# Expert stage: residual and pair sums on TensorE, weights split 2048 columns at a time

## The chip, the cores and the metric

The kernel runs on one core of one Trainium2 chip. The metric is device time in microseconds of one execution; several executions are timed and the median is given. PE is TensorE, DVE is VectorE, ACT is ScalarE, POOL is GpSimd, SP is SyncE, which here issues the loads of weights.

## The reference

A block of two layers on x of 256 tokens x 1024 channels, in float32. Each layer adds a mixer (retention, latent attention, mLSTM), then a feed-forward part, each with a residual and a layer norm. The second layer's feed-forward part is a mixture of 8 experts, of which each token takes 2:

```python
logits = (t @ router).astype(jnp.float32)
top_v, top_i = lax.top_k(logits, TOP_K)
top_w = jax.nn.softmax(top_v, axis=-1)
gate = jnp.sum(jax.nn.one_hot(top_i, N_EXPERTS) * top_w[..., None], axis=1)
y = jnp.zeros((bsz * s, d), jnp.float32)
for e in range(N_EXPERTS):
    y = y + gate[:, e:e + 1] * swiglu(t, wg[e], wu[e], wd[e])
...
x = layer_norm(DN_ALPHA * x + f, ln2_w[l], ln2_b[l])
```

swiglu is (silu(x @ wg) * (x @ wu)) @ wd with a hidden width of 3584. The experts' weights are 352 MB in float32. Everything else is small beside them.

## The kernel before, in words

**Numbers in two parts.** PE multiplies fp32r values. To keep float32's precision each operand is split into a high part (a cast to fp32r, by ACT) and a low part (operand minus high part, by DVE). A product is then three matmuls (`mm3`, L374: high x high, high x low, low x high). Where an expert has at most 64 tokens, high and low part of the activations stand side by side in the 128 columns of one stationary operand, and two matmuls do (`products`, L1544, the branch at L1564); a small matmul (`fold_in`, L1590) then adds the low half to the high one. Which of the two ways an expert takes is decided on the chip by its token count.

**Weights.** A piece is 128 partitions x 2048 columns (1 MB), loaded by SP into a raw place. `piece` (L313) returns a function `half(i)` that splits 1024 of its columns: one ACT cast (L347) and one DVE subtract (L348) into a pair of places from `next_pair` (L358). `Feed` (L225) holds the order: reading half n emits the split of all halves up to n + `feed.conv` (L267), so the splits run ahead of PE by a fixed number. In the mixers and the dense part six pair places of 8 KB per partition take turns. In the expert stage (`MHM` = 4) four of them go on taking turns, `feed.conv` is 3, and the other two become raw places ("wp"). The raw places there are listed in `WHERE` (L62): 4 in the ring, 5 in "e1r", 2 "wp", 2 "eb", 13 in all, reused in turn; three more (`ONCE`) are used once at the start. The last 8 pieces (`FINE`) are cut into 512 columns, and the very last one (`quarters`, L1277) too.

**The loop.** `UNITS` runs over experts in pairs (0,1), (2,3), (4,5), (6,7), and in each expert over 7 slices of 512 hidden columns. One turn of the loop (L1710) is a unit of 6 pieces: gate (2 pieces), up (2 pieces), and the down projection of the unit before (2 pieces). Between them stand, in an order written out by hand for ACT and DVE (`manual_schedule`, L1708): the copy of the low half (`lower`, L1585), silu (`hidden`, L1601), its product with up (`hidden_times`, L1605), and the split of the transposed hidden block hT (`turn`, L1608, split at L386 and L387). PE's order is written out by hand throughout. Tasks that are less pressing (gathering the next pair's tokens, preparing its way back, an expert's way back) are generators from which `little` (L1536) takes one step at a few points of each unit.

**An expert's way back.** When an expert's 7 slices are summed in two PSUM banks z, `scatter` (L1655) scales them by the gate (ACT L1663 for the high part, DVE L1664 for the low part, into zb), multiplies them with the transposed one-hot matrix (8 matmuls at L1670, two for each of 4 banks of 128 tokens x 512 channels), and DVE adds each bank to x_sb (L1675; for the last expert L1677, with a running sum for the layer norm). x_sb starts as ALPHA times the residual, which POOL builds from the parts xh and xl in unit (0, 2) with four operations (L1751, L1752). After the last expert a check for overfull experts (L1773) and the layer norm follow.

Of the kernel before, what the change touches and what calls it, by code (L numbers as in the profile page):

```python
# [11 lines left out]
F32 = mybir.dt.float32  # L12
# [22 lines left out]
T1, T2, M2 = 6, 5, 2  # L35
MHL, MHM = 6, 4
NEB = 2
# [29 lines left out]
HALF = CAP // 2  # L67
GAPS = 32, 160, 160
SGM, HTB, OHB = 2, 1, 1
# [202 lines left out]
def tile_hybrid_block(  # L272
# [39 lines left out]

    def piece(src, a, b, by_col=False, pair=None, raw=None, cut=None, fine=False):  # L313


        if raw == "big":
            w = big([PIECE], F32)
        else:
            pl, n = raw or (ring, NRING)
            tag, n = (n, 1) if isinstance(n, str) else ("w", n)  # L320
            w = pl.tile([P, PIECE], F32, tag=tag, bufs=n, name="w")
        wv = w[:, :a * b].rearrange("p (a b) -> p a b", a=a)
        if fine:
            for i in range(a):
                sp.dma_start(wv[:, i], src[:, i])
        elif cut is None:
            sp.dma_start(wv, src)
        else:

            sp.dma_start(wv[:, :a // 2], src[:, :a // 2])  # L330
            cut.append(lambda: sp.dma_start(wv[:, a // 2:], src[:, a // 2:]))

        def half(i):
            if by_col:
                a_, b_ = a, b // 2
                src_ = wv[:, :, i * b_:(i + 1) * b_]
            else:
                a_, b_ = a // 2, b
                src_ = wv[:, i * a_:(i + 1) * a_]
            hv, lv = [q[:, :a_ * b_].rearrange("p (a b) -> p a b", a=a_) for q in (pair or next_pair)()]  # L340
            with ExitStack() as st:
                for i_ in feed.behind if feed.done > feed.free else ():
                    st.enter_context(tc.issue_after(i_))
                if feed.done - 1 in KEEP:
                    st.enter_context(tc.issue_after(next(j for j in reversed(nc.cur_bb.bb.instructions) if j.engine == dve.engine)))
                for c in ([(slice(None), j) for j in range(a_)] if a_ > 1 else [(slice(None), slice(None), slice(j * 512, j * 512 + 512)) for j in range(2)]) if fine else [slice(None)]:
# [62 lines left out]

    def rstd_of(mp, dst, var, n, more=None):  # L410

        v = mp.tile([P, n], F32, tag="rs_v", bufs=3, name="rs_v")
        t_ = mp.tile([P, n], F32, tag="rs_t", bufs=3, name="rs_t")
        if more is None:
            dve.tensor_scalar(v, var, EPS, None, op0=OP.add)
        else:
            dve.tensor_scalar(v, var, more, EPS, op0=OP.add, op1=OP.add)  # L417
        dve.tensor_scalar(dst.bitcast(I32), v.bitcast(I32), -0.5, magic, op0=OP.mult, op1=OP.add)  # L418
# [825 lines left out]
    def moe_weights():  # L1244
        count, spare = [0], [0]
        of_moe = lambda: next_pair(True)

# [8 lines left out]
        def add(src, a, b):  # L1256
            where = place()
            fine = count[0] > 6 * len(UNITS) - FINE
            if where in ONCE:
                feed.add(lambda pl: piece(src, a, b, raw=(pl, "x" if where == "xp" else XG[ORDER[1][int(where[2])]]), pair=of_moe, fine=fine), place=where)  # L1260
            elif where == "wp":
                spare[0] += 1
                feed.add(lambda pl, i=spare[0] % (MHL - MHM): piece(src, a, b, raw=(pl, routes["spare"][i]), pair=of_moe, fine=fine), place=where)
            elif where:
                feed.add(lambda pl: piece(src, a, b, raw="big" if where == "eb" else (pl, WHERE.count(where)), pair=of_moe, fine=fine), place=where)
            else:
                feed.add(lambda: piece(src, a, b, pair=of_moe, fine=fine))

# [8 lines left out]
        def quarters(w):  # L1277
# [4 lines left out]
            for h in range(2):  # L1282
                for k in range(2):
                    sp.dma_start(tv[:, k, h], wv[:, k, h])

            def half(h):
                hv, lv = [q.rearrange("p (k n) -> p k n", k=2) for q in next_pair(True)]
                for k in range(2):
# [123 lines left out]
    def moe(mp, free_order):  # L1412
# [24 lines left out]

        def gates():
            for t in range(2):
                lg, m8 = lgs[t]  # L1440
                nm = mp.tile([P, 1], F32, tag="nm", bufs=2, name="nm")
                gs = mp.tile([P, 1], F32, tag="gs", bufs=2, name="gs")
# [3 lines left out]
                dve.reciprocal(gs, gs)  # L1446
                dve.tensor_scalar(gate[:, t], gate[:, t], gs, None, op0=OP.mult)

        def fullest():

            mxr = mp.tile([2 * NE, 1], F32, tag="mxr", name="mxr")
            mxf = mp.tile([1, 1], F32, tag="mxf", name="mxf")
            cnt = mp.tile([1, NE], F32, tag="cnt", name="cnt")
# [78 lines left out]
        hs = {}  # L1532
        gapped = []
        tasks = []
# [73 lines left out]
        def turn(e, s, joined=False):  # L1608
# [21 lines left out]
            else:  # L1630
                if not gapped:
                    gap(mp, GAPS[1], "gap1")
                hT = mp.tile([P, 4, 2, P], F32R, tag="hT", bufs=HTB, name="hT")
                if not gapped:
                    gapped.append(gap(mp, GAPS[2], "gap2"))
            hs[e, s] = hT
# [3 lines left out]
        def down(e, s, after={}, few={}):  # L1640
# [3 lines left out]
            for j in range(2):  # L1644
                pw = feed.next()
                last = (e, s, j) == (*UNITS[-1], 1)
                for i in range(2):
# [5 lines left out]
                    after.get(2 * j + i, lambda: None)()  # L1653

        def scatter(e, sums=None):  # L1655

            _, ohT, gsl = state.pop(e)
            zz = z.pop(e)
            zb = mp.tile([P, 2, 2, 512], F32R, tag=XG[e], name="zb")

# [4 lines left out]

            def back(t, h, whole=None):
                ps = bank()
                if whole is None:
                    for part in range(2):
                        pe.matmul(ps, ohT[:, t * P:(t + 1) * P], zb[:, h, part], start=(part == 0), stop=(part == 1))  # L1670
                else:
                    pe.matmul(ps, ohT[:, t * P:(t + 1) * P].bitcast(F32), whole, start=True, stop=True)
                ys = x_sb[:, t, h * 512:(h + 1) * 512]
                if sums is None:
                    dve.tensor_tensor(ys, ys, ps, op=OP.add)  # L1675
# [3 lines left out]
            if sums is None:  # L1679
# [3 lines left out]
                soon_all()  # L1683
                for t in range(2):
                    for h in range(2):
                        back(t, h)
                    yield
            else:
                scale(0)
                zf = mp.tile([P, 512], F32, tag="sgm", bufs=SGM, name="zf")  # L1690
                act.mul(zf, zz[1], gsl)
                for t in range(2):
                    back(t, 0)
                for t in range(2):
                    back(t, 1, zf)

# [11 lines left out]
        inner.enter_context(tc.manual_schedule(engines={mybir.EngineType.Activation, mybir.EngineType.DVE}))  # L1708
        feed.conv = MHM - 1
        for i_, (e, s) in [(i // (2 * NS), u) for i, u in enumerate(UNITS)]:  # L1710
# [31 lines left out]
            else:  # L1742
# [22 lines left out]
        down(*prev)  # L1765
        sums = [mp.tile([P, 2], F32, tag="sums", bufs=2, name="sums") for _ in range(2)]
        for _ in scatter(prev[0], sums):
# [65 lines left out]
        xc = big([2, D], F32)  # L1833
        var = [mp.tile([P, 2], F32, tag="lnvar", bufs=2, name="lnvar") for _ in range(2)]
        for t in range(2):
# [9 lines left out]
        for t in range(2):  # L1845
            rs = mp.tile([P, 1], F32, tag="lnrs", bufs=2, name="lnrs")
            rstd_of(mp, rs, var[t][:, :1], 1, var[t][:, 1:])
            norm_shift(t, rs, lb, xc[:, t], lambda c: sp.dma_start(ov[:, t, c], x_sb[:, t, c]))
# [25 lines left out]
    with phase("e1", "right") as mp:  # L1874
        feed.places["e1"] = feed.places["eb"] = feed.places["xg0"] = feed.places["xg1"] = mp
        feed.places["wp"], feed.places["xp"] = whl, xpool
        moe(mp, order.close)
# [45 lines left out]
```

## Time and profile before

The median of 3 runs is 1412.47 us (1411.46 to 1412.53).

| | us |
|---|---|
| profiled execution | 1411.74 |
| its span, first to last instruction | 1410.0 |
| PE busy | 1360.8 (97%) |
| DVE busy | 1235.0 (88%) |
| ACT busy | 1049.0 (74%) |
| POOL busy | 57.3 (4%) |

The expert stage begins at about 457 us and its loop ends at about 1392 us. The span in 40 equal slices, busy share in tenths (PEclk is the granted clock of TensorE in tenths of full speed, DMA the busy share of the 16 DMA engines):

```profile
PE   9999999999999989999999999999999999999995
DVE  7998645468878999999999899998999999999996
ACT  7743534435642889999888889988888898998884
PEclk9999999999999999999999999999999999999998
DMA  9363836563258979999999999999999999999951
```

A row of the windows view reads: start and end of the stretch in us, its length, then busy us and number of instructions (x) of PE, PEld (PE's weight loads), DVE, ACT and POOL, then the granted clock, the busy share of the DMA engines and GB/s. Where it was asked for one line of the code, it has that line's engine alone. A row of the order of time reads: start, us from the first start to the last end, engine, line, operation, out<-in, shapes, count of neighbours merged, and in brackets the idle time before with what ended it. The landing of a load (last number of its row) is in us from its issue.

Busy time of matmuls is modelled and says little on how near PE is to its peak. What an engine waited for, and which engine has no idle time, is read stage by stage.

### The profile page before, as it was taken

How to read it: one execution, taken by the hardware profiler on the slowest of the kernel's cores; microseconds unless marked ns; L12 is line 12 of the kernel's file. 1: busy time of each engine (PE TensorE's matmuls, PEld its weight loads, DVE VectorE, ACT ScalarE, POOL GpSimd, SP SyncE). 2: the span in 40 equal slices, each digit the busy share in tenths (PEclk: the TensorE clock that was granted, in tenths of full speed). 3: DMA queues.
4: the chain of work that ended last, by engine and by line, in shares of the span. 5: the costliest groups of instructions: out<-in, count | busy, mean ns of one | idle time of the engine just before them, and what ended most of it. 6: DMA issues, size and time to landing. Idle time of an engine off the chain costs nothing. (4 is left out here: it accounts for less than half of the span.)

```text
span 1410.0 us, 20525 instructions
## 1 busy us (share of the span) xinstructions
PE 1360.8 (97%) x7017; PEld 1086.4 (77%) x7017; DVE 1235.0 (88%) x1702; ACT 1049.0 (74%) x1384; POOL 57.3 (4%) x70
## 2 busy tenths in 40 slices
PE   9999999999999989999999999999999999999995
PEld 8887999988888856656788865678888886667884
DVE  7998645468878999999999899998999999999996
ACT  7743534435642889999888889988888898998884
POOL 1021000001021040000000000000000000000000
PEclk9999999999999999999999999999999999999998
DMA  9363836563258979999999999999999999999951
GB/s 345 123 226 129 269 120 210 197 211 126 88 181 321 368 267 383 400 379 404 402 392 361 349 382 392 403 403 388 349 362 353 364 375 381 393 403 402 378 215 38
DMA packets 200044, 431.17 MB, mean 306 GB/s; under 512 B 9824, under 2 KB 44000, under 8 KB 199904
## 3 DMA queue, kind: packets, MB, share of 16 engines
q1 hardware_dynamic: 195952, 425.01, 81.9%
q0 software_dynamic: 864, 3.15, 0.6%
q8 instruction: 92, 1.51, 0.4%
q10 hardware_dynamic: 3088, 1.11, 0.3%
q14 instruction: 48, 0.39, 0.1%
HBM read 428.19 MB, written 1.05 MB: 304 GB/s over the span
## 5 line engine op out<-in xcount | busy, mean ns | idle before, releaser
L348 DVE TENSOR_TENSOR wp<-w,wp 128x1024 fp32r<-128x1024 f32 (+2 forms) x676 | 785.5, 1201 | 103.8 <-ACT wp L347 100.0
L347 ACT CAST wp<-w 128x1024 fp32r<-128x1024 f32 (+2 forms) x676 | 678.6, 1030 | 157.7 <-PE pm L383 35.7
L1567 PE MATMUL pm<-wp,xg 128*128 128x512 f32 x848 | 225.2, 409 | 19.3 <-DVE wp L348 18.3
L1567 PEld LDWEIGHTS pm<-wp,xg 128*128 128x128 f32 x848 | 151.2, 190 | 78.8 <-DVE wp L348 49.4
L377 PE MATMUL pm<-wp,xg 128*128 128x512 f32 x472 | 184.9, 392 | 3.5 <-DVE wp L348 3.5
L376 PE MATMUL pm<-wp,xg 128*128 128x512 f32 x472 | 186.8, 396 | 0.0
L378 PE MATMUL pm<-wp,xg 128*128 128x512 f32 x472 | 184.2, 390 | 0.0
L1567 PE MATMUL z<-wp,hT 128*128 128x512 f32 x448 | 129.1, 417 | 1.1 <-DVE wp L348 1.1
L348 DVE TENSOR_TENSOR wp<-big,wp 128x1024 fp32r<-128x1024 f32 x100 | 118.5, 1217 | 6.1 <-ACT wp L347 5.1
L347 ACT CAST wp<-big 128x1024 fp32r<-128x1024 f32 x100 | 102.5, 1050 | 11.1 <-PE pm L378 7.7
L1567 PEld LDWEIGHTS z<-wp,hT 128*128 128x128 f32 x448 | 75.8, 188 | 42.2 <-DVE wp L348 21.8
L377 PEld LDWEIGHTS pm<-wp,xg 128*128 128x128 f32 x472 | 88.8, 188 | 23.7 <-DVE wp L348 6.4
L378 PEld LDWEIGHTS pm<-wp,xg 128*128 128x128 f32 x472 | 88.6, 188 | 18.5
L376 PEld LDWEIGHTS pm<-wp,xg 128*128 128x128 f32 x472 | 88.7, 188 | 17.8
L381 PE MATMUL pm<-big,wp 128*128 128x256 f32 x320 | 90.6, 283 | 0.0
L383 PE MATMUL pm<-big,wp 128*128 128x256 f32 x320 | 90.6, 283 | 0.0
L382 PE MATMUL pm<-big,wp 128*128 128x256 f32 x320 | 90.5, 283 | 0.0
L376 PE MATMUL z<-wp,hT 128*128 128x512 f32 x216 | 85.0, 393 | 0.0
L377 PE MATMUL z<-wp,hT 128*128 128x512 f32 x216 | 84.4, 391 | 0.4 <-DVE wp L348 0.4
L378 PE MATMUL z<-wp,hT 128*128 128x512 f32 x216 | 84.1, 389 | 0.0
L520 PE MATMUL pm<-wp,big 128*128 128x512 f32 (+1 forms) x288 | 69.9, 390 | 1.2 <-DVE wp L348 0.6
L1588 ACT CAST low<-pm 64x512 fp32r<-64x512 f32 x109 | 63.5, 583 | 2.7
(323 smaller groups left out, 1842.2 us busy)
## 6 DMA issues: line engine op xcount, KB each, us to landing
w<-in_moe_w_gate_dram SPq DMA_DIRECT2D x93, 1024.0 KB, 8.4
w<-in_moe_w_up_dram SPq DMA_DIRECT2D x93, 1024.0 KB, 7.8
w<-in_moe_w_down_dram SPq DMA_DIRECT2D x92, 1024.0 KB, 7.8
big<-in_moe_w_gate_dram SPq DMA_DIRECT2D x17, 1024.0 KB, 7.4
big<-in_moe_w_up_dram SPq DMA_DIRECT2D x17, 1024.0 KB, 8.2
w<-in_w_in_dram SPq DMA_DIRECT2D x16, 1024.0 KB, 8.9
big<-in_moe_w_down_dram SPq DMA_DIRECT2D x16, 1024.0 KB, 9.4
w<-in_ffn_w_gate_dram SPq DMA_DIRECT2D x11, 1024.0 KB, 5.8
```

Of the source, the lines that this page charges most:

```text
L347: act.copy(hv[c], src_[c])
L348: dve.tensor_tensor(lv[c], src_[c], hv[c].bitcast(F32), op=OP.subtract)
L376: pe.matmul(ps, s[0], m[0], start=first, stop=False)
L377: pe.matmul(ps, s[0], m[1], start=False, stop=False)
L378: pe.matmul(ps, s[1], m[0], start=False, stop=last)
L381: pe.matmul(ps, s[0], m[0], start=first, stop=False)
L382: pe.matmul(ps, s[1], m[0], start=False, stop=False)
L383: pe.matmul(ps, s[0], m[1], start=False, stop=last)
L520: pe.matmul(o, s, m, start=start, stop=stop)
L1567: pe.matmul(ps, both, m[part], start=begin and part == 0, stop=last and part == 1)
L1588: act.copy(low[0][HALF:], ps[HALF:])
```

## The change

Three things change together in the expert stage.

- **A piece is split at once.** `half(0)` of a piece splits all 2048 columns with one cast and one subtract; `half(1)` only returns the second part. `next_whole` takes two of the six 8 KB places, one for the high part and one for the low part, so that there are three places of 16 KB. `feed.conv` becomes 4: reading the first half of piece n emits the split of piece n + 2. The two "wp" raw places go, and `WHERE` has 11.
- **Sums on PE.** The two experts of a pair are sent back together, at the second one's end: for each of the 4 banks the products of both experts accumulate in PSUM, and DVE adds once. For the first pair a matmul of xl with an identity (`eye`) opens each bank, and DVE's add takes xh as its other operand, so that x_sb = xh + (xl + results). POOL's four operations go.
- **No ALPHA.** Instead of scaling the residual by ALPHA, the gates are scaled by 1/ALPHA, and the last layer norm uses EPS / ALPHA^2.

Besides, small tiles share tags, and the unused gaps between tiles go. The diff, cut to its core:

```diff
-WHERE = [None] * 4 + ["e1r"] * 5 + ["wp"] * (MHL - MHM) + ["eb"] * NEB
+WHERE = [None] * 4 + ["e1r"] * 5 + ["eb"] * NEB
...
+        both = []
+
         def half(i):
+            if at_once:
+                if i == 0:
+                    both[:] = split_into(next_whole(), a, b, wv)
+                return [q[:, i * (a // 2):(i + 1) * (a // 2)] for q in both]
...
-    def next_pair(moe=False):
-        if moe and len(pairs) > MHM:
-
-            routes["spare"] = ["wp%d" % i for i in pairs[MHM:]]
-            del pairs[MHM:]
+    def next_whole():
+
+        two = pairs[:2]
+        pairs[:] = pairs[2:] + two
+        return [whl.tile([P, PIECE], F32R, tag="wp%d" % i, bufs=1, name="wp") for i in two]
...
-                dve.tensor_scalar(gate[:, t], gate[:, t], gs, None, op0=OP.mult)
+                dve.tensor_scalar(gate[:, t], gate[:, t], gs, 1 / ALPHA, op0=OP.mult, op1=OP.mult)
...
+                    eye.append(mp.tile([P, P], F32R, tag="eye", name="eye"))
+                    act.copy(eye[0], ident)
...
+            def add(ps, t, h):
+                c = slice(h * 512, (h + 1) * 512)
+                ys = x_sb[:, t, c]
+                if two == ORDER[0]:
+                    dve.tensor_tensor(ys, xh[:, t, c].bitcast(F32), ps, op=OP.add)
+                elif sums is None:
                     dve.tensor_tensor(ys, ys, ps, op=OP.add)
...
-                for t in range(2):
-                    for h in range(2):
-                        back(t, h)
+                if e == two[1]:
+                    new_x(two)
+                    for t in range(2):
+                        for h in range(2):
+                            ps = bank()
+                            if two == ORDER[0]:
+                                pe.matmul(ps, eye[0], xl[:, t, h * 512:(h + 1) * 512], start=True, stop=False)
+                            for e_ in two:
+                                back(e_, ps, t, h, e_ == two[0] and two != ORDER[0], e_ == e)
+                            add(ps, t, h)
+                            if h and t == 0:
+                                yield
                     yield
             else:
                 scale(0)
                 zf = mp.tile([P, 512], F32, tag="sgm", bufs=SGM, name="zf")
                 act.mul(zf, zz[1], gsl)
-                for t in range(2):
-                    back(t, 0)
-                for t in range(2):
-                    back(t, 1, zf)
+                todo = [(t, h, bank()) for h in range(2) for t in range(2)]
+                for t, h, ps in todo:
+                    back(two[0], ps, t, h, True, False)
+                for t, h, ps in todo:
+                    back(e, ps, t, h, False, True, zf if h else None)
+                    add(ps, t, h)
...
-        feed.conv = MHM - 1
+        feed.conv = 4
...
-            if (e, s) == (0, 2):
-
-                x_sb = xpool.tile([P, 2, D], F32, tag="x", name="x_sb")
-                for t in range(2):
-                    pool.tensor_tensor(x_sb[:, t], xh[:, t].bitcast(F32), xl[:, t].bitcast(F32), op=OP.add)
-                    pool.tensor_scalar(x_sb[:, t], x_sb[:, t], ALPHA, None, op0=OP.mult)
```

## Rows read from the trace of the kernel before

**Rows 1.** Windows, one per run of experts (914.59 to 1158.68 left out)

```profile
475.92:682.70 206.78, 193.77 (x818) 130.19 (x817) 205.66 (x200) 188.05 (x221) 15.57 (x4) 0.98 0.98 369
682.70:807.13 124.43, 123.26 (x579) 101.84 (x578) 114.15 (x118) 105.78 (x125) 0.00 (x0) 1.00 1.01 374
807.13:914.59 107.46, 103.63 (x423) 67.44 (x422) 107.46 (x105) 100.24 (x115) 0.00 (x0) 1.00 1.03 390
...
1158.68:1266.80 108.12, 104.14 (x436) 69.20 (x435) 107.76 (x108) 100.91 (x117) 0.00 (x0) 1.00 1.04 392
1266.80:1382.33 115.53, 114.35 (x518) 93.38 (x518) 108.53 (x115) 100.63 (x124) 0.00 (x0) 1.00 0.83 313
```

**Rows 2.** Windows of units: few tokens, many tokens, scalings, POOL

```profile
638.24:653.06 14.82, 14.29 (x59) 9.07 (x58) 14.82 (x16) 14.03 (x17) 0.00 (x0) 1.00 1.04 403
1108.28:1125.08 16.80, 16.80 (x78) 13.92 (x77) 15.45 (x16) 14.75 (x16) 0.00 (x0) 1.00 1.00 348
821.95:840.48 18.53, 17.61 (x74) 11.81 (x72) 18.53 (x22) 16.87 (x20) 0.00 (x0) 1.00 1.02 383
507.17:527.46 20.29, 16.88 (x59) 11.01 (x58) 20.29 (x16) 14.04 (x17) 12.38 (x4) 0.83 0.83 284
```

**Rows 3.** Order of time, DVE, few-token unit at 638

```profile
638.24 0.68 DVE L1606 TENSOR_TENSOR sgm<-sgm,pm 128x512 f32<-128x512 f32 x1
638.84 1.22 DVE L348 TENSOR_TENSOR wp<-w,wp 128x1024 fp32r<-128x1024 f32 x1
639.97 4.62 DVE L348 TENSOR_TENSOR wp<-big,wp 128x1024 fp32r<-128x1024 f32 x4
```

**Rows 4.** Groups by form, expert stage: count, busy us, mean ns, idle before

```profile
L348 DVE TENSOR_TENSOR wp<-w,wp 128x1024 fp32r<-128x1024 f32 x549 | 649.0, 1226 | 30.8 <-ACT wp L347 27.1 <-DMA w<-in_moe_w_up_dram 0.5
...
L347 ACT CAST wp<-w 128x1024 fp32r<-128x1024 f32 x548 | 559.8, 1050 | 59.8 <-PE pm L378 31.0 <-PE pm L1567 15.3 <-PE z L378 4.5
...
L348 DVE TENSOR_TENSOR wp<-w,wp 128x512 fp32r<-128x512 f32 x28 | 17.5, 685 | 1.0 <-ACT wp L347 1.0
...
L347 ACT CAST wp<-w 128x512 fp32r<-128x512 f32 x28 | 15.7, 618 | 1.3 <-PE pm L378 1.1
```

**Rows 5.** Windows of L348 alone, the three runs that DVE fills

```profile
475.92:682.70 206.78, 185.45 (x156) 0.98 0.98 369
807.13:914.59 107.46, 96.58 (x85) 1.00 1.03 390
1158.68:1266.80 108.12, 96.90 (x85) 1.00 1.04 392
```

**Rows 6.** DVE and POOL in order of time, unit at 507

```profile
507.77 11.21 DVE L348 TENSOR_TENSOR wp<-w,wp 128x1024 fp32r<-128x1024 f32 x5
...
503.98 8.83 POOL L1751 TENSOR_TENSOR x_sb<-big 128x1024 f32<-128x1024 f32 x2 [48.61 <-DVE wp L348]
```

**Rows 7.** DVE in order of time, unit at 822: scalings, first two adds

```profile
822.55 1.40 DVE L1664 SCALAR_TENSOR_TENSOR zb<-z,gsl,zb 128x512 fp32r<-128x512 f32 x2
...
828.40 1.27 DVE L1675 TENSOR_TENSOR x_sb<-x_sb,pm 128x512 f32<-128x512 f32 x2
```

**Rows 8.** PE in order of time: expert 0's way back, and the last expert's

```profile
593.82 1.09 PE L1670 MATMUL pm<-zb,ohT 128*128 128x512 f32 x4
...
1391.86 0.39 PE L378 MATMUL z<-wp,hl 128*128 128x512 f32 x1
1392.09 1.33 PE L1670 MATMUL pm<-zb,ohT 128*128 128x512 f32 x4
1393.26 1.88 PE L1672 MATMUL pm<-zf,ohT 128*128 128x512 f32 x4
```

**Rows 9.** DMA view, 623 to 683 us, then landing in 1039 to 1158

```profile
DMA packets 10264, 23.90 MB, mean 403 GB/s; under 512 B 361, under 2 KB 361, under 8 KB 10259
...
w<-in_moe_w_gate_dram SPq DMA_DIRECT2D x8, 1024.0 KB, 11.4
...
w<-in_moe_w_gate_dram SPq DMA_DIRECT2D x13, 1024.0 KB, 6.3
```

More of the change, by code (lines that the diff above doesn't have):

```diff
@@ L311, in tile_hybrid_block, with piece @@
     magic = float(0x5F3759DF)
-    def piece(src, a, b, by_col=False, pair=None, raw=None, cut=None, fine=False):
+    def piece(src, a, b, by_col=False, pair=None, raw=None, cut=None, fine=False, at_once=False):
         if raw == "big":
@@ L1244, in moe_weights @@
     def moe_weights():
-        count, spare = [0], [0]
-        of_moe = lambda: next_pair(True)
+        count = [0]
         def place():
@@ L1259, in add @@
             if where in ONCE:
[L1260 to L1263, printed above, removed]
+                feed.add(lambda pl: piece(src, a, b, raw=(pl, "x" if where == "xp" else XG[ORDER[1][int(where[2])]]), at_once=True, fine=fine), place=where)
             elif where:
-                feed.add(lambda pl: piece(src, a, b, raw="big" if where == "eb" else (pl, WHERE.count(where)), pair=of_moe, fine=fine), place=where)
+                feed.add(lambda pl: piece(src, a, b, raw="big" if where == "eb" else (pl, WHERE.count(where)), at_once=True, fine=fine), place=where)
             else:
-                feed.add(lambda: piece(src, a, b, pair=of_moe, fine=fine))
+                feed.add(lambda: piece(src, a, b, at_once=True, fine=fine))
         def whole(w, s_):
@@ L1532, in moe @@
         hs = {}
-        gapped = []
+        gapped, eye = [], []
         tasks = []
@@ L1653, in down @@
                     after.get(2 * j + i, lambda: None)()
+        zbs = {}
         def scatter(e, sums=None):
-            _, ohT, gsl = state.pop(e)
+            two = next(p for p in ORDER if e in p)
+            gsl = state[e][2]
             zz = z.pop(e)
-            zb = mp.tile([P, 2, 2, 512], F32R, tag=XG[e], name="zb")
+            zb = zbs[e] = mp.tile([P, 2, 2, 512], F32R, tag=XG[e], name="zb")
             def scale(h):
@@ L1664, in scale, with back @@
                 dve.scalar_tensor_tensor(zl, zz[h], gsl, zh.bitcast(F32), op0=OP.mult, op1=OP.subtract)
-            def back(t, h, whole=None):
-                ps = bank()
+            def back(e_, ps, t, h, first, last, whole=None):
+                ohT = state[e_][1][:, t * P:(t + 1) * P]
                 if whole is None:
                     for part in range(2):
-                        pe.matmul(ps, ohT[:, t * P:(t + 1) * P], zb[:, h, part], start=(part == 0), stop=(part == 1))
+                        pe.matmul(ps, ohT, zbs[e_][:, h, part], start=first and part == 0, stop=last and part == 1)
                 else:
-                    pe.matmul(ps, ohT[:, t * P:(t + 1) * P].bitcast(F32), whole, start=True, stop=True)
-                ys = x_sb[:, t, h * 512:(h + 1) * 512]
-                if sums is None:
+                    pe.matmul(ps, ohT.bitcast(F32), whole, start=first, stop=last)
+            def add(ps, t, h):
[4 more added lines that the diff above has]
+                elif sums is None:
                     dve.tensor_tensor(ys, ys, ps, op=OP.add)
@@ L1765, in moe @@
         down(*prev)
-        sums = [mp.tile([P, 2], F32, tag="sums", bufs=2, name="sums") for _ in range(2)]
+        sums = [mp.tile([P, 2], F32, tag=n, name="sums") for n in ("mxr", "mxf")]
         for _ in scatter(prev[0], sums):
@@ L1833, in moe @@
         xc = big([2, D], F32)
-        var = [mp.tile([P, 2], F32, tag="lnvar", bufs=2, name="lnvar") for _ in range(2)]
+        var = [mp.tile([P, 2], F32, tag="nm", bufs=2, name="lnvar") for _ in range(2)]
         for t in range(2):
```

43 lines of the change are left out of this document (27 added, 16 removed).

## The prediction

> **What bounds the kernel now.** I read the page first (PE busy 97%, DVE 88%, no engine plainly the limit), then one row per run of experts [rows 1]. The expert stage falls into two kinds of run. In the runs at 475.92, 807.13 and 1158.68 (experts 0 and 1, 3, and 6, at most 64 tokens each: two matmuls per product, L1567) DVE is busy for 420.9 of 422.4 us: it has no idle time to speak of. In the other three (experts 2, 4 and 5, and 7: three matmuls, L376 to L378; the first and the last are shown) PE is busy for all but 1.2 us of each run. I then took one unit (512 columns of one expert's hidden width, 6 pieces of weights) of each kind [rows 2]: the few-token unit takes 14.82 us with DVE at 14.82; the many-token unit 16.80 us with PE at 16.80 and DVE idle 1.35. So time leaves the first kind only by taking work off DVE, and enters the second only by work put on PE (or by making PE wait).
>
> Third, DVE in order of time in the few-token unit [rows 3]: 12 subtracts of 1024 columns (L348) and two operations of 512 columns. Four in a row take 4.62 us and one takes 1.22, so start to start is (4.62 - 1.22) / 3 = 1.135 us; the end of one overlaps the next. 12 x 1.135 + 2 x 0.60 = 14.82: the unit is exactly DVE's list of work.
>
> **The change part by part.**
>
> *A piece split in one go.* Start to start, DVE takes 0.60 us for 512 columns and 1.135 for 1024 [rows 3], 0.535 per 512, so 0.065 of each instruction is not columns. A 2048-column subtract should be followed after 1.135 + 2 x 0.535 = 2.205 us, against 2.27 for two halves. The lone durations say the same: 2 x 0.685 - 1.226 = 0.144 [rows 4], less the 1.22 - 1.135 by which neighbours overlap, is 0.06. The three DVE-bound runs hold 156 + 85 + 85 = 326 subtracts [rows 5], 163 pieces: 163 x 0.065 = **-10.6 us**. Bounds: 0, if DVE comes to wait, and -12, if a piece saves the 0.073 that 2.20 would give. I take the middle reading, since that is how DVE runs there. A few-token unit becomes 6 x 2.205 + 1.20 = 14.4 us. In the PE-bound runs the same saving falls into DVE's idle time and is worth nothing. The last 8 pieces stay cut into 512 columns.
>
> *Does the coarser piece still arrive?* Three whole places replace four half places, so piece n+2 is split when PE is done with n-1. The cast of 2048 columns lasts about 1.050 + 0.864 = 1.91 us (0.432 per 512 [rows 4]), the subtract 1.22 + 1.07 = 2.29. In the few-token unit I laid the steady state out by hand: DVE in the order U0, U1, D0, hT, D1, G0', G1', product (G, U, D: gate, up, down; ' the next unit). D0's 8 matmuls wait for hT (ready 7.3 us after U0's subtract began) and, 0.23 us apart [rows 8], are done at 9.5; G1' takes D0's place, so its cast ends at 11.4, and DVE wants it at 11.6. Every other cast has 0.6 us or more. So DVE stays full, with 0.2 us to spare at the tightest point. In the many-token unit PE gives 2 pieces x 12 x 0.227 = 5.4 us of cover (a unit of 16.80 less its transposes, over 72 matmuls), the chain needs 1.91 + 2.29 + some 0.3 to be released: 0.9 us to spare (with half pieces: 3 x 6 x 0.227 = 4.1 against 1.05 + 1.22 + 0.3 = 2.6). Nothing is charged, but this is where it can fail.
>
> *The residual no longer on POOL.* In the unit at 507.17, DVE needs 20.29 us for a list that takes 14.82 elsewhere [rows 2]: five subtracts last 11.21 us together instead of 5.76, and just then POOL runs the four operations that build x_sb (L1751 and L1752; two are shown [rows 6]). They go, and nothing replaces them on DVE: **-5.5 us** (the bounds are 0 and the same 5.5; PE's clock is at 0.83 in that unit, but DVE, which has no such clock, sets its length). DVE's first pair of sums now reads xh and the bank, of the same size as before.
>
> *Sums per pair instead of per expert.* An expert's way back is 2 scalings and 4 adds on DVE [rows 7]; the four adds take 4 x 0.60 = 2.4 us. They disappear for experts 0, 2, 4, 6. Those of 0 and 2 run inside DVE-bound runs (that of 2 at 822 [rows 7]): **-4.8 us**. Those of 4 and 6 run in PE-bound ones: nothing.
>
> *PE.* Eight back products per expert, 0.23 us apart ((1.09 - 0.39) / 3 [rows 8]), 1.84 us, now run at the pair's end. Expert 0's leave a DVE-bound run and enter a PE-bound one (+1.84, and 4 products with the identity, +0.9); expert 2's likewise (+1.84); expert 4's leave a PE-bound run for expert 6's DVE-bound one (-1.84; there PE's 8 more lie in a unit that DVE's scalings and adds lengthen by 3.7 us, as at 821.95 [rows 2], and are covered); expert 6's leave one (-1.84) for the very end. Sum **+0.9**. At the end, 8 products stand ahead of the last expert's, where PE now goes on without a gap at 1392.09 and waits only some 0.3 us before 1393.26 [rows 8]: 1.84 - 0.25 = **+1.6**.
>
> *Raw places.* 13 become 11 in the ring of loads. SP issues a load when DVE has freed a place. In the DVE-bound run at 623 the loads land 403 GB/s, a median of 11.4 us after issue; the unit eats 6.29 MB in 14.82 us, 424 GB/s [rows 9]. So a stock is being run down. In a PE-bound run a place comes round every 11 x 2.8 = 31 us, of which 6.3 is transfer and some 4.5 split: 20 us of stock. A run of 7 units at 14.4 needs 42 pieces in 101 us and gets one per 2.6 us: 8.3 us of stock used, 12 left. The first run has DVE's extra work between its pieces (gathers, a way back) and uses about 10. Cost 0.
>
> The eye tile (one small ACT copy), 1/ALPHA in the gates and eps / ALPHA^2 cost nothing that can be seen: ACT has 0.8 us idle in the few-token unit [rows 2].
>
> **Sum:** -10.6 - 5.5 - 4.8 + 0.9 + 1.6 = -18.4. The profiled execution took 1411.7 us (span 1410.0); the median of the runs shown is 0.7 higher, within their spread. 1412.2 - 18.4 = **1393.8 us**.
>
> **Rivals.**
>
> *A. DVE loses its fullness.* The 0.2 us at D0 is not there: a low-half copy or a latency stands in the way, DVE waits about 0.4 us per few-token unit, and the 10.6 are gone: 1404. For it: ACT is busy 14.03 of 14.82 us there [rows 2], so it has little room to catch up. Against: its list gets shorter by up to 6 x (2 x 1.050 - 1.914) = 1.1 us per unit [rows 4].
>
> *B. PE waits in the many-token units* (slower). Here DVE is not full, so long pieces save nothing and make each result come later. Place: the second matmul of a piece, which needs the subtract. If ACT or DVE has an operation of 0.6 us in front twice (silu and the low copy on ACT, product and hT on DVE), the 0.9 us is used up; 28 units x 6 pieces x 0.15 us = 25 us: 1418. It decides the sign from 18.4 / 168 = 0.11 us per piece. Against: the late ones do not add up, since DVE's idle 1.35 per unit takes them back, and by the order of the code the 0.6 us operations are spread over different pieces. The Trainium skill (Perfetto Trace Analysis, Optimizing Scalar/DVE Operations) states both halves of this: grouping helps a saturated engine, and breaking up helps where an unsaturated one causes bubbles on another. By the second half alone the change loses in the PE-bound runs; no row here shows such a bubble yet.
>
> *C. The loads become the bound* (slower at worst). Without stock a few-token unit takes 6.29 MB / 403 GB/s = 15.6 us, 1.2 more than forecast, and 27 units give at most +32: 1425; if the stock ends only in the last third of each run, +10: 1403. Against: the stock worked out above. The Trainium skill (DMA: Bandwidth & Descriptors, Specifications) gives about 358 GB/s of HBM per core and 435 GB/s for the fabric. By the first, the units would already be load-bound at 17.6 us, which the 403 GB/s row contradicts; by the second, 14.4 us is just at the ceiling (436), and no run here has shown that rate.
>
> *D. No effect:* DVE's saving is given back by the PE blocks at the pair ends and at the end. These are 4.6 and 1.6 us; it would take another 14 that I find nowhere.
>
> **How the numbers follow.** Forecast 0.68 (its own range 1388 to 1398: -12 for the subtracts, a lead of one more piece at each of three entries to a DVE-bound run, or 4 us of small waits); A 0.15 (1398 to 1407); B 0.08; C 0.06, half of it slower; D 0.03 (1409 to 1415). A difference under 0.2% (2.8 us) can't be told from none. Faster 0.86, same 0.04, slower 0.10. Range 1388 to 1405, which leaves out B, D, the worse half of C, the tail of A and a little below.
>
> **What would show it.** Right: few-token units of 14.4 us between two L1606 with no DVE idle; subtracts of 2048 columns near 2.29 us and 2.2 apart; the unit after POOL's as short as its neighbours and no POOL work; many-token units still 16.8; 4 adds per pair. Wrong: DVE idle before L348, released by ACT, in the few-token units (A); PE or its loads idle on L348 in the many-token ones (B); DVE or ACT released by a landing (C).

## The result, and the profile after

The changed kernel takes **1392.84 us** (median of 4 runs, 1392.49 to 1394.05), the kernel before 1412.5 in the same session: a ratio of 0.9863 (95% interval 0.9846 to 0.988). Run once more later it took 1392.69 (0.9859, 0.9844 to 0.9874). The forecast was 1393.8. The two medians are 19.7 us apart.

The profiled execution has a span of 1391.2 us. Its runs of experts, in the windows view with the columns of [rows 1]:

```profile
475.96:670.55 194.59, 183.52 (x807) 131.05 (x806) 192.52 (x119) 179.44 (x143) 0.00 (x0) 0.99 1.00 386
670.55:796.94 126.39, 126.36 (x593) 104.61 (x592) 111.09 (x75) 99.48 (x83) 0.00 (x0) 1.00 1.02 378
796.94:899.54 102.60, 96.33 (x413) 67.48 (x412) 102.36 (x59) 95.60 (x73) 0.00 (x0) 1.00 1.04 397
899.54:1143.02 243.48, 243.44 (x1122) 201.21 (x1122) 216.13 (x133) 196.51 (x155) 0.00 (x0) 1.00 1.01 378
1143.02:1248.59 105.57, 101.13 (x441) 72.24 (x440) 105.05 (x65) 96.32 (x75) 0.00 (x0) 1.00 1.03 389
1248.59:1362.52 113.93, 113.26 (x512) 92.33 (x511) 103.92 (x80) 95.05 (x93) 0.00 (x0) 1.00 0.89 339
```

Set beside [rows 1], and beside the prediction's terms sorted by run (the last row of before is cut 0.7 us short of the last product of silu and up; here both are taken up to it):

| run | before | after | change | predicted |
|---|---|---|---|---|
| experts 0, 1 (few tokens) | 206.8 | 194.6 | -12.2 | -13.0 |
| 2 (many) | 124.4 | 126.4 | +2.0 | +2.7 |
| 3 (few) | 107.5 | 102.6 | -4.9 | -5.2 |
| 4, 5 (many) | 244.1 | 243.5 | -0.6 | 0 |
| 6 (few) | 108.1 | 105.6 | -2.5 | -2.8 |
| 7 (many) | 116.2 | 113.9 | -2.3 | -1.8 |
| from there to the end | 27.0 | 28.7 | +1.7 | +1.6 |

The unit windows that answer to [rows 2], in its order: few tokens, many tokens, scalings (now without adds), and the unit at which POOL had worked.

```profile
627.33:641.73 14.40, 13.43 (x59) 9.37 (x58) 14.40 (x9) 13.44 (x11) 0.00 (x0) 1.00 1.04 411
1092.62:1109.42 16.80, 16.80 (x78) 13.91 (x77) 14.87 (x10) 13.73 (x11) 0.00 (x0) 1.00 1.01 376
811.64:827.50 15.86, 14.60 (x64) 10.31 (x63) 15.82 (x11) 15.31 (x12) 0.00 (x0) 1.00 1.03 384
506.75:521.15 14.40, 13.45 (x59) 9.38 (x58) 14.40 (x9) 13.44 (x11) 0.00 (x0) 1.00 1.04 398
```

In the plain units shown DVE still has no idle time with few tokens, and PE none with many. DVE in order of time in the former [rows 3], and the groups by form [rows 4]:

```profile
641.73 0.68 DVE L1618 TENSOR_TENSOR sgm<-sgm,pm 128x512 f32<-128x512 f32 x1
642.33 6.69 DVE L357 TENSOR_TENSOR wp<-w,wp 128x2048 fp32r<-128x2048 f32 x3
648.94 0.68 DVE L398 TENSOR_TENSOR hT<-pm,hT 128x512 fp32r<-128x512 f32 x1
649.54 6.69 DVE L357 TENSOR_TENSOR wp<-w,wp 128x2048 fp32r<-128x2048 f32 x3
```

```profile
L357 DVE TENSOR_TENSOR wp<-w,wp 128x2048 fp32r<-128x2048 f32 x269 | 609.4, 2287 | 46.0 <-ACT wp L356 43.4 <-DMA w<-in_moe_w_up_dram 0.9 <-DMA big<-in_moe_w_gate_dram 0.4
L356 ACT CAST wp<-w 128x2048 fp32r<-128x2048 f32 x267 | 507.1, 1910 | 77.1 <-PE pm L389 47.8 <-PE z L389 11.1 <-PE pm L1603 7.5
```

A subtract of 2048 columns lasts 2.287 us, and is followed after (6.69 - 2.287) / 2 = 2.20: 6 x 2.20 + 2 x 0.60 = 14.4. One row of ACT shows how close a cast came to being late: the one at 651.89 (G1', the piece that takes D0's place) begins when PE has freed its place (0.42 us idle) and ends at 653.80; DVE begins the subtract that needs it at 649.54 + 2 x 2.20 = 653.94, 0.14 us later.

```profile
651.89 1.91 ACT L356 CAST wp<-w 128x2048 fp32r<-128x2048 f32 x1 [0.42 <-PE z L1579]
```

### The profile page after: what moved, and what is told of

The parts are those of the page before. It is cut to its first block, busy times and chain, and to the rows that moved or that the text cites. A ratio compares the mean times of both kernels' runs of the same rounds, so it can differ in the third digit from the quotient of the medians.

```text
span 1391.2 us, 19646 instructions
## 1 busy us (share of the span) xinstructions
PE 1344.7 (97%) x7021; PEld 1094.9 (79%) x7021; DVE 1195.2 (86%) x1358; ACT 1004.8 (72%) x1057; POOL 41.8 (3%) x66
## 3 DMA queue, kind: packets, MB, share of 16 engines
HBM read 428.19 MB, written 1.05 MB: 309 GB/s over the span
## 5 line engine op out<-in xcount | busy, mean ns | idle before, releaser
L357 DVE TENSOR_TENSOR wp<-w,wp 128x2048 fp32r<-128x2048 f32 (+3 forms) x382 | 734.6, 1944 | 116.4 <-ACT wp L356 113.6
L356 ACT CAST wp<-w 128x2048 fp32r<-128x2048 f32 (+3 forms) x382 | 618.4, 1632 | 170.8 <-PE pm L389 48.3
L357 DVE TENSOR_TENSOR wp<-big,wp 128x2048 fp32r<-128x2048 f32 (+1 forms) x66 | 136.9, 2093 | 9.9 <-ACT wp L356 9.1
L1579 PE MATMUL z<-wp,hT 128*128 128x512 f32 x448 | 117.2, 403 | 17.8 <-DVE hT L398 15.6
L356 ACT CAST wp<-big 128x2048 fp32r<-128x2048 f32 (+1 forms) x66 | 115.0, 1757 | 13.7 <-PE pm L389 10.0
L1579 PEld LDWEIGHTS z<-wp,hT 128*128 128x128 f32 x448 | 80.0, 188 | 44.7 <-issue 25.9
L387 PE MATMUL z<-wp,hT 128*128 128x512 f32 x216 | 85.0, 393 | 0.0
L389 PE MATMUL z<-wp,hT 128*128 128x512 f32 x216 | 84.3, 390 | 0.2
L388 PE MATMUL z<-wp,hT 128*128 128x512 f32 x216 | 84.2, 390 | 0.0
```

The costliest lines, as they stand in the source:

```text
L387: pe.matmul(ps, s[0], m[0], start=first, stop=False)
L388: pe.matmul(ps, s[0], m[1], start=False, stop=False)
L389: pe.matmul(ps, s[1], m[0], start=False, stop=last)
L1579: pe.matmul(ps, both, m[part], start=begin and part == 0, stop=last and part == 1)
```

## The experiments

Each starts from the changed kernel unless it is said. The kernel before is run beside each.

**e1_subs, e2_casts: undo the merging in one engine.**

```diff
                     act.copy(hv[c], src_[c])
-                    dve.tensor_tensor(lv[c], src_[c], hv[c].bitcast(F32), op=OP.subtract)
+                    for c_ in [c] if fine or not at_once else [(slice(None), slice(i * a_ // 2, (i + 1) * a_ // 2)) for i in range(2)]:
+                        dve.tensor_tensor(lv[c_], src_[c_], hv[c_].bitcast(F32), op=OP.subtract)
```

(e2_casts has the loop around the cast instead.)

> The changed kernel (1392.8 us), but each piece's subtract is again two subtracts of 1024 columns; cast, places and order stay whole. Theory (DVE's list of instructions is the length of a few-token unit): 12 x 1.135 + 2 x 0.60 = 14.82 instead of 14.41, 0.41 more in each of some 24 units that DVE fills, so about +10 us: 1403; the many-token units keep 16.8. Rival (the gain came from the whole places or from ACT's shorter list): no more than +2 us, and the units keep about 14.4.

> The changed kernel, but each piece's cast is again two casts of 1024 columns; the subtract stays whole. Theory: ACT's list in a few-token unit grows by 6 x (2 x 0.95 - 1.83) = 0.4 us of its 0.96 us idle, and the tightest cast in the trace ends 0.14 us before DVE wants it; two casts end 0.95 + 1.05 - 1.91 = 0.09 later, so DVE stays nearly full: 0 to +2 us, 1393 to 1395. Rival (ACT is the hidden bound, as in rival A of the prediction): DVE waits 0.4 us in each few-token unit, the units are 14.8 again and the time is about 1403.

e2_casts: 1393.23 us, no change; ACT's idle time in a few-token unit falls from 0.96 to 0.5 and DVE stays full. e1_subs: **1412.3**, ratio to before 1.0007 (0.9998 to 1.0016). Undoing half of the merging alone gives back everything: twice what the theory expected, and far more than the rival's 2 us. The windows view of two neighbouring few-token units, of a stretch in the first, and of a third unit of the same trace:

```profile
835.72:851.71 15.99, 14.21 (x57) 10.39 (x57) 14.92 (x16) 13.07 (x10) 0.00 (x0) 0.89 1.04 401
851.71:866.52 14.81, 13.42 (x61) 9.94 (x60) 14.81 (x15) 13.75 (x12) 0.00 (x0) 1.00 1.04 406
843.97:848.48 4.51, 4.51 (x13) 3.29 (x13) 4.39 (x4) 1.76 (x3) 0.00 (x0) 0.62 1.05 400
602.27:617.08 14.81, 13.03 (x60) 9.60 (x59) 14.81 (x15) 13.35 (x11) 0.00 (x0) 1.00 1.04 409
```

The second and the third unit have the 14.82 that the theory gives. The first is 1.2 us longer, with DVE idle for 1.07 and a granted clock of 0.62 in the stretch shown. PE's rows of the three units, then ACT's and DVE's of the first, in order of time:

```profile
843.97 4.58 PE L1580 MATMUL z<-wp,hT 128*128 128x512 f32 x12 [1.78 <-DVE hT L399]
...
859.95 3.00 PE L1580 MATMUL z<-wp,hT 128*128 128x512 f32 x12 [1.39 <-DVE hT L399]
...
610.57 3.00 PE L1580 MATMUL z<-wp,hT 128*128 128x512 f32 x12 [1.78 <-DVE hT L399]
```

```profile
847.50 1.90 ACT L356 CAST wp<-w 128x2048 fp32r<-128x2048 f32 x1 [2.72 <-issue]
...
849.43 2.36 DVE L358 TENSOR_TENSOR wp<-w,wp 128x1024 fp32r<-128x1024 f32 x2 [1.07 <-ACT wp L356]
```

In the first unit PE waits 1.78 us for the low part of hT. The granted clock is still 1.00 during the wait (842.20 to 843.97); after it PE runs mostly at 1.2 GHz and not at 2.4, and the same 12 matmuls take 4.58 us instead of 3.00. The cast into D0's place begins 3.5 us after the first of them, where the third unit has 2.2 (612.74 after 610.57), and DVE stands still. The third unit is the comparison that matters: its wait is as long, 1.78 us, but its clock stays at 1.00, and the unit is no longer than the list. It is the place with the margin of 0.14 us from above that gives way. Nine few-token units of this trace have a half clock; they are 0.8 to 1.4 us longer than the list gives, 9.6 us together; with 0.41 in each of some 24 units that makes 19.4, and the medians are 19.5 apart.

**e9_busy: e1_subs with PE kept busy.** Four matmuls that add zero to z stand ahead of D0's products in the few-token branch.

```diff
+                             ([lambda: [pe.matmul(z[e][n % 2][:HALF], fold[:HALF], pw[0][0][:HALF, 0, :512], start=False, stop=False, skip_group_check=True) for n in range(4)]] if s and j == i == 0 else (), ()),
```

> Two subtracts of 1024 columns per piece as in e1_subs (1412.3 us), and before the down projection's first products of a few-token unit PE runs four more matmuls that add zero (0.9 us), in the time in which it waits for hT. In e1_subs that wait was 1.4 to 1.8 us, and in about every second unit the granted clock was at half behind it and DVE then waited about 1 us for a place. Theory (the 9 us beyond the subtracts' own 10 come from TensorE's clock falling after its longer wait): no half clock in these units, every few-token unit about 14.8, 1402 to 1404. Rival (the waits of the whole places with slower subtracts cost that by themselves, and the clock only shows them): 1412 or more, since PE has more to do.

**1403.94 us** (ratio 0.995, 0.9933 to 0.9966). PE in order of time, and two neighbouring units:

```profile
853.11 1.13 PE L1669 MATMUL z<-wp,fold 64*64 64x512 f32 x4
855.35 3.00 PE L1580 MATMUL z<-wp,hT 128*128 128x512 f32 x12 [1.11 <-DVE hT L399]
```

```profile
847.11:861.93 14.82, 13.71 (x63) 9.88 (x62) 14.82 (x15) 13.34 (x11) 0.00 (x0) 1.00 1.04 405
861.93:876.75 14.82, 13.78 (x63) 9.96 (x63) 14.82 (x15) 13.43 (x11) 0.00 (x0) 1.00 1.04 403
```

More work for PE made the kernel 8.4 us faster: the clock stays at 1.00 in every unit of the loop, every plain few-token unit is 14.82, and DVE has no idle time in it. So the clock was the cause, not a sign. What is left, 1403.9 - 1392.7 = 11.2 us, comes with the second subtract: unit by unit against the second trace of the changed kernel, 10.0 us in the few-token runs (24 x 0.41 = 9.8) and 1.5 in the others, nearly all of it in the first unit of each many-token run.

**e8_halves: only the coarse places left.** The loop of e1_subs stands around cast and subtract together.

```diff
-                    act.copy(hv[c], src_[c])
-                    dve.tensor_tensor(lv[c], src_[c], hv[c].bitcast(F32), op=OP.subtract)
+                    for c_ in [c] if fine or not at_once else [(slice(None), slice(i * a_ // 2, (i + 1) * a_ // 2)) for i in range(2)]:
+                        act.copy(hv[c_], src_[c_])
+                        dve.tensor_tensor(lv[c_], src_[c_], hv[c_].bitcast(F32), op=OP.subtract)
```

> Whole places and the changed order, but cast and subtract of each piece again in two of 1024 columns each, so that only the coarse release of places is left of the whole pieces. Theory (DVE's list is longer by 0.41 us per few-token unit, hT's low part comes later for PE, and the clock falls): about as e1_subs, 1408 to 1414. Rival (in e1_subs the long cast ahead of a short subtract made the trouble): every few-token unit 14.8 and no half clock, 1402 to 1404.

**1401.59 us** (0.9927, 0.991 to 0.9943): 0.4 us below the rival's range and far from the theory's, though the clock falls as often as in e1_subs (ten stretches against nine), which the rival did not expect. Seven of the ten such units are no longer than 14.82 us, as this one with a granted clock of 0.88. Its window, then PE and ACT in order of time:

```profile
658.86:673.68 14.82, 13.03 (x52) 9.31 (x52) 14.82 (x16) 12.43 (x16) 0.00 (x0) 0.88 1.04 409
```

```profile
667.10 4.58 PE L1580 MATMUL z<-wp,hT 128*128 128x512 f32 x12 [1.79 <-DVE hT L399]
...
670.04 1.99 ACT L357 CAST wp<-w 128x1024 fp32r<-128x1024 f32 x2 [1.73 <-PE z L1580]
```

The place is as late as in e1_subs, but with casts by halves DVE can begin when half a piece is cast. The first half is done at 670.04 + 1.05 = 671.09, and DVE begins its subtract at 671.41, right behind the one before; a cast of the whole piece would have ended at 671.95. In these seven units a half clock cost nothing in itself, since PE isn't the bound there; in e1_subs it cost what it made late.

**e3_pool: POOL's four operations put back** into unit (0, 2), where nothing waits for them.

```diff
+            if (e, s) == (0, 2):
+                x_sb = xpool.tile([P, 2, D], F32, tag="x", name="x_sb")
+                for t in range(2):
+                    pool.tensor_tensor(x_sb[:, t], xh[:, t].bitcast(F32), xl[:, t].bitcast(F32), op=OP.add)
+                    pool.tensor_scalar(x_sb[:, t], x_sb[:, t], ALPHA, None, op0=OP.mult)
```

> The changed kernel with POOL's four operations on x_sb put back into unit (0, 2); what they write is overwritten later by the first pair's sums, and nothing waits for it. Theory (POOL's operations lengthen DVE's subtracts): the unit that is 14.41 becomes about 19.9, +5.5 us: 1398.3; the subtracts of 2048 columns beside POOL last about twice as long. Rival 1 (PE's half clock made that unit long, and was there for another reason): 0. Rival 2 (it was the wait for x_sb): 0, since nothing waits for it here.

**1396.47 us**. The two units that POOL touches last 19.06 and 14.65 us, 4.9 more than 2 x 14.41. Windows, then DVE and POOL in order of time:

```profile
491.10:510.16 19.06, 14.42 (x60) 9.21 (x58) 19.06 (x9) 14.86 (x12) 13.75 (x4) 1.00 0.57 195
510.16:524.81 14.65, 13.47 (x57) 9.37 (x58) 14.65 (x9) 12.30 (x11) 2.71 (x1) 1.00 1.02 362
```

```profile
498.91 11.33 DVE L357 TENSOR_TENSOR wp<-w,wp 128x2048 fp32r<-128x2048 f32 x3
...
496.32 8.72 POOL L1789 TENSOR_TENSOR x_sb<-big 128x1024 f32<-128x1024 f32 x2 [41.02 <-DVE wp L357]
505.13 7.74 POOL L1790 TENSOR_SCALAR x_sb<-x_sb 128x1024 f32<-128x1024 f32 x2
```

Three subtracts last 11.33 us where three last 6.69. The clock is at 1.00 throughout, so rival 1 is out: POOL's work makes that unit long without a half clock. The median moved by 3.6 and not 4.9; this trace lacks two half-clock stretches that the changed kernel's has (below), which fits, but was not tried by itself.

**e4_each and s1_sums: the sums on PE, undone and alone.** In e4_each every expert is sent back by itself; s1_sums is the kernel before with the change's scatter, gates and last norm alone: sums on PE, no work on POOL, pieces split by halves into 13 raw places. Its edit puts the splitting of the kernel before (`piece`, `next_pair`, `WHERE`, `feed.conv`) back into the changed kernel; shown is the core of e4_each's.

```diff
-                if e == two[1]:
+                if True:
...
-                            for e_ in two:
-                                back(e_, ps, t, h, e_ == two[0] and two != ORDER[0], e_ == e)
+                            back(e, ps, t, h, e != ORDER[0][0], True)
```

> The changed kernel, but each expert's results are sent back and added by itself, as in the kernel before (the residual's low part still enters through the identity, with expert 0). By the accounts of the two traces, run by run: first run +1.7, second -1.6, third +2.3, fourth -0.7 + 1.8, last run +2.2, end -1.75: about +4 us, 1396.8. By the prediction's own terms (4.8 for the adds, -0.9 and -1.6 for PE): +2.3 us, 1395.1. Rival (the adds had been hidden): 0 or a gain of 1.6 at the end, 1391 to 1393.

> One part alone: the kernel before with the sums on PE and without POOL's four operations; pieces are split by halves into half places as before (13 raw places). By the prediction's terms -5.5 -4.8 +0.9 +1.6 = -7.8 us against the kernel before: 1404. Units of 14.82, no half clock in them. Rival (as in e8_halves, where the same cast and subtract by halves stood in whole places: 1401.6): below 1402, if the whole places help by themselves; above 1406, if the sums on PE are worth nothing here either, as e4_each suggests (then only POOL's 4 to 5.5 us are gained).

s1_sums: **1405.3 us** (0.9948, 0.9935 to 0.9962), -7.1 against the -7.8 of the terms. Two of its units: the one where POOL had been (20.29 before) and the one with expert 2's adds (18.53 before):

```profile
508.62:523.44 14.82, 14.29 (x59) 9.07 (x58) 14.82 (x16) 14.02 (x17) 0.00 (x0) 1.00 1.00 365
818.99:835.12 16.13, 15.58 (x66) 10.23 (x64) 16.13 (x17) 16.01 (x19) 0.00 (x0) 1.00 1.02 380
```

Unit by unit: -5.46 where POOL had been, -2.39 at expert 2's adds, +2.75, +1.84, -1.82 and -1.81 where back products enter or leave a PE-bound run, and +1.35 at the end; all other units keep their length within 0.04. Only expert 0's adds gave -1.72 instead of -2.4: that unit has a half clock.

s1_sums and the changed kernel differ by the whole pieces alone, so their loops, from first unit to last, give that step in its place. Each has one half clock after expert 0. The loop of s1_sums lasts 898.46 us (477.36 to 1375.82), that of the changed kernel 886.56 (475.96 to 1362.52). That is -11.9 us, where the prediction has -10.6. e8_halves, with whole places but halves in them, has a loop of 897.5 us: the coarse places by themselves are worth about 1 us (with ten half clocks in the loop), the long instructions in them the rest.

e4_each: **1393.0**, so the rival's time. By runs, against the second trace of the changed kernel: +2.3, -2.7, +2.4, 0, +0.1, +1.1 and -1.6 at the end, +1.7 in all; the loop of e4_each's trace happens to start 1.8 us earlier (below), so the medians hide it. Beside whole pieces the pair sums are thus worth little. My +4 came from differences between before and after that held another effect as well, which the next run shows.

**w1_whole: the whole pieces alone**, with POOL's operations and each expert by itself.

```diff
...
-                            if two == ORDER[0]:
-                                pe.matmul(ps, eye[0], xl[:, t, h * 512:(h + 1) * 512], start=True, stop=False)
-                            for e_ in two:
-                                back(e_, ps, t, h, e_ == two[0] and two != ORDER[0], e_ == e)
+                            back(e, ps, t, h, True, True)
...
+            if (e, s) == (0, 2):
+                x_sb = xpool.tile([P, 2, D], F32, tag="x", name="x_sb")
...
```

> The other part alone: the changed kernel's whole pieces, while each expert is sent back by itself and POOL builds the residual's sum in unit (0, 2) (its factor is 1 here, since the gates are scaled). By the prediction's term -10.6 us against the kernel before: 1401.2. By what the single undoings cost (e3_pool +3.6, e4_each +0.2, on 1392.8): 1396.6 to 1398. Rival (the whole pieces need the shorter list that the other parts give, as they needed the single subtract): above 1404, with half clock in few-token units.

**1398.52 us**, -13.9 against its kernel before (0.9906, 0.9891 to 0.9921): 2.7 us below what the prediction's term gives, and 0.5 above the range from the single undoings. Its plain few-token units save 0.41 each. By units of the two traces the loop is 13.2 us shorter, and 2.6 of that come from the many-token runs, above all from units with an expert's way back: first the kernel before, then w1_whole.

```profile
698.86:717.76 18.90, 17.73 (x80) 14.34 (x80) 18.62 (x22) 15.48 (x17) 0.00 (x0) 1.00 1.04 410
```

```profile
692.39:710.50 18.11, 18.11 (x83) 15.02 (x82) 18.11 (x15) 14.84 (x11) 0.00 (x0) 1.00 1.04 405
```

In three such units (experts 1, 3 and 6) PE had waited 1.17 us, since DVE with two scalings and four adds on top was all but full there (18.62 of 18.90); a shorter list gives 0.8 us back, and 0.3 to 0.4 in the next unit.

**e5_places9, e5_places8: how near are the loads?**

```diff
-WHERE = [None] * 4 + ["e1r"] * 5 + ["eb"] * NEB
+WHERE = [None] * 4 + ["e1r"] * 3 + ["eb"] * NEB
```

(2 instead of 3 for eight places.)

> The changed kernel with 9 raw places in the ring of loads instead of 11. In its trace the shortest time from a piece's landing to its cast is 2.7 us at the end of the first few-token run, 3.6 and about 4.3 in the other two, and a place is worth 2.4 us of DVE's time there. Theory (the stock at the end is 2.7 us, one place): two places less lack 2.1 us in the first run, 1.2 in the second and 0.5 in the third, +3 to +5 us: 1396 to 1398. Rival (the prediction's own account, 12 us of stock left): 0, 1392 to 1393.5.

> The changed kernel with 8 raw places instead of 11. Theory (stock of one place left): three places are 7.2 us, so 4.5, 3.6 and 2.9 us are lacking in the three few-token runs: +11 us or a little more, 1402 to 1406. Rival (the prediction's account, 12 us left): 0 to +1.

**1392.48 and 1394.42 us.** Nine places cost nothing, eight 1.7 us. Both theories fell, and for a plain reason: I had paired each landing with the cast of the piece two further back. Paired rightly, the shortest time from a landing to its cast in the expert stage is 8.05 us with 11 places and 0.35 with nine, both near 657 us, at the end of the first few-token run. With eight ACT waits for landings in the last units of the first run; one of its rows, and one such unit:

```profile
644.79 1.91 ACT L356 CAST wp<-big 128x2048 fp32r<-128x2048 f32 x1 [0.65 <-DMA big<-in_moe_w_down_dram]
```

```profile
641.27:656.88 15.61, 13.95 (x60) 9.30 (x58) 14.80 (x10) 13.61 (x11) 0.00 (x0) 1.00 1.04 400
```

**m1_mix and the changed kernel again.** m1_mix sends the experts of the first and the last pair back one by one.

```diff
-                if e == two[1]:
+                apart = two in (ORDER[0], ORDER[-1])
+                if apart or e == two[1]:
...
-                            for e_ in two:
+                            for e_ in (e,) if apart else two:
```

> The changed kernel, with the experts of the first and the last pair sent back one by one and those of the two middle pairs together. From the units of e4_each against the changed kernel's: first pair +2.4 -2.8, last pair +1.1 -1.5, together -0.8 us: 1392, and no half clock in the unit that follows expert 0. Rival (the differences of single units don't add up): 1392.8 or more.

> The changed kernel once more, beside the others on the same chip: 1392.8, within 1 us. If a half clock near 457 us or in the unit at 582 us comes and goes between executions, a trace without them has a span shorter by up to 1.9 us.

**1391.53 us** (0.9851, 0.9837 to 0.9864) and **1392.69** (0.9859, 0.9844 to 0.9874). By runs m1_mix has +2.4, -2.8, +1.1 and -1.5, the expected -0.8; the medians alone can't tell the two apart. The median of m1_mix is the lowest measured here.

## Why the prediction was right

The forecast is 1.0 us from the measured time, and the terms that carry it were found where it had put them. That it came so near is in part luck: some 1.9 us vary between executions (below), and two effects that it did not have, one of some 2.7 us and one of some 2.0, nearly cancel.

**A piece split in one go: -10.6 predicted.** In the few-token units right to 0.02 us: 14.41 against 6 x 2.205 + 1.20 = 14.43. By itself the step is worth more, -11.9 by the loops above and -13.9 in w1_whole, since "in the PE-bound runs the same saving falls into DVE's idle time and is worth nothing" doesn't hold in the three units with a way back. In the changed kernel that gain shows too: expert 0's products and the identity's cost +1.6 at 687 and not +2.7, expert 2's +0.7 and not +1.8; with expert 6's unit that is some 2.7 us. Against it stands a loss that I hadn't charged. With whole pieces the first unit of a many-token run is 0.46 us longer than before, and the first of a few-token run is shorter by 0.12 only and not by 0.41; over three such changes and two back some 2.0 us. PE is busy for all of the longer unit, with 76 or 77 matmuls in it instead of 75, so it enters the run further behind; what puts it there was not tried. The two nearly cancel. First the kernel before, then two units of the changed one:

```profile
682.70:698.86 16.16, 16.16 (x75) 12.67 (x74) 15.19 (x15) 14.10 (x18) 0.00 (x0) 1.00 1.04 395
...
670.55:687.17 16.62, 16.59 (x77) 12.86 (x76) 14.82 (x10) 13.50 (x13) 0.00 (x0) 1.00 1.04 401
687.17:707.64 20.47, 20.47 (x94) 16.94 (x93) 18.38 (x15) 14.57 (x11) 0.00 (x0) 1.00 1.04 404
```

The Trainium skill (Perfetto Trace Analysis, Optimizing Scalar/DVE Operations) says that larger operations help a saturated engine, and that breaking up may help where an unsaturated one causes bubbles on another. The first half agrees (0.41 us per unit). The second would have spoken against the change in the many-token units; the plain one shown above is 16.80 as before.

**Does the coarser piece arrive: 0.2 us to spare.** Measured 0.14. That it was "where it can fail" was right, and how it fails was not foreseen: not by 0.4 us of waiting in each unit, but through TensorE's clock, at 0.8 to 1.4 us in each of the units that it hits (e1_subs, a later edit; the changed kernel itself keeps its margin). Rival A had the place, not the mechanism. Rival B did not happen: PE is busy for all of a many-token unit.

**The residual no longer on POOL: -5.5.** -5.46 in s1_sums; 4.9 with whole pieces (e3_pool).

**Sums per pair: -4.8, PE +0.9 and +1.6.** Confirmed term by term in s1_sums (the end is +1.35 there). Within the changed kernel, where back products meet units that the shorter list has already relieved, they are worth 1.7 by units instead of the 2.3 of these terms. The end: 8 + 4 products in a row, then the last ones (L1692, of which the view has three of four).

```profile
1372.02 2.88 PE L1690 MATMUL pm<-zb,ohT 128*128 128x512 f32 x12
1374.74 1.45 PE L1692 MATMUL pm<-zf,ohT 128*128 128x512 f32 x3
```

**Raw places: cost 0, 12 us of stock left.** Cost 0 is right. The stock is smaller: 8.05 us at the end of the first run, for which the prediction had some 10, and 8.9 to 9.1 in the other two. The 20 us that it starts from were right (20.0 in the run at 797); 11 of them are used there and not 8.3. The rate is what it was [rows 9], 405 GB/s, and the median landing of gate's pieces is 11.9 us where it was 11.4:

```profile
DMA packets 9743, 23.48 MB, mean 405 GB/s; under 512 B 355, under 2 KB 355, under 8 KB 9737
...
w<-in_moe_w_gate_dram SPq DMA_DIRECT2D x7, 1024.0 KB, 11.9
```

So rival C is three places away (e5_places8), and a further microsecond taken off DVE in the long few-token run would be paid from 8 us of stock.

**One thing missing from the sum** is a half clock in the unit after expert 0, which comes and goes. First the profile of the changed kernel, then its second one:

```profile
582.11:598.51 16.40, 15.24 (x60) 10.59 (x58) 15.91 (x12) 14.39 (x11) 0.00 (x0) 0.90 1.04 399
```

```profile
582.62:598.35 15.73, 13.59 (x59) 9.38 (x58) 15.73 (x12) 14.54 (x12) 0.00 (x0) 1.00 1.05 400
```

That is 0.67 us. The loop's start moves too: 474.1 to 475.0 us in the five traces of whole-piece kernels without a half clock near 457 us, 475.9 to 476.6 in the seven with one. Some 1.9 us thus vary between executions, and single traces had to be compared unit by unit.

## What to carry to other kernels

Where one engine's list fills a stage, price an edit by start-to-start times on that engine, and check the units in which another engine is named as the bound but has idle time: there the list counts as well. Lay the steady state out by hand to find the tightest hand-over: here it told not only whether the change works, but which later edit breaks it. An engine that isn't the bound can still lose time for all, if its clock falls after a wait and what it frees comes late.

## What the hardware showed

- Matmuls of 512 columns that followed a wait of 1.78 us ran mostly at 1.2 GHz (12 in 4.58 us, e1_subs at 843.97); behind a wait as long, at 610.57 of the same trace, they ran at 2.4 GHz (3.00). So the length of a wait doesn't decide: in the changed kernel's unit at 582 the clock fell after 1.16 us (the row below), and in the long unit of e3_pool PE was idle for 19.06 - 14.42 = 4.6 us in all and the clock stayed. What does is left open here. Four useless matmuls in each few-token unit's wait (1.1 us) kept it up and made e1_subs 8.4 us faster.

```profile
586.37 5.06 PE L1579 MATMUL pm<-wp,xg 128*128 128x512 f32 x14 [1.16 <-DVE wp L357]
```

- Four POOL operations of 128x1024 cost DVE 4.9 us, 1.2 each, more than the 1.135 us [rows 3] that DVE takes for such an operation itself. The Trainium skill (Perfetto Trace Analysis, Optimizing Scalar/DVE Operations) warns that moving work between the two "might not help"; here it costs.
